# One split of the output weights, four quarter passes, and a norm bank of its own

## The chip, the cores and the metric

The kernel runs on one core of one Trainium2 chip. The metric is the device time of one execution in microseconds. The kernel before takes 2251.65 us, the median of three runs (2248.07 to 2252.68). The engines are called by their usual names: TensorE (PE) multiplies matrices, VectorE (DVE), ScalarE (ACT) and GpSimd (POOL) work on elements, and SyncE (SP) issues most of the transfers.

## The reference, cut to what matters

It is one layer of a decoder for 1024 prompt tokens and 8 sample tokens, model width 1024, feed-forward width 2816:

```
mix = (sigmoid(ga) * y_a + sigmoid(gb) * y_b) @ w_o
x   = x + gt1 * mix
h2  = rmsnorm(x, norm2_w) * (1 + sc2) + sh2
gate, up = h2 @ w_ffn_gate, h2 @ w_ffn_up
gc  = causal_dwconv3(gate with its state) + ffn_conv_b
x   = x + gt2 * ((silu(gc) * up) @ w_ffn_down)
y   = rmsnorm(x, final_norm_w)
```

Ahead of these lines come the modulation from the conditioning, one combined input projection, a gated delta rule (its output times w_gdn_out is y_a) and sliding-window attention (its output times w_swa_out is y_b). All numbers are float32.

## The kernel before

Every matrix lies transposed on the chip, channels on the 128 partitions and tokens along the row, so a matrix of width 1024 is 8 blocks of channels. To keep float32 accuracy, every operand is split in a high part, rounded by ScalarE (`split`, L126), and a low part, the rest, from VectorE (L127); a product is three matmuls (`mm3`, L168 high by high, L169 high weight by low operand, L170 low weight by high operand). A weight block is 1024 rows by 128 columns: `load_w` loads its 512 KB into one of three buffers called raw and splits it in two tiles of 128x1024.

The tokens are cut in three parts for the branches (`PARTS`), and in four quarters of 256, 256, 260 and 260 columns behind them (`QUARTERS`); quarters 0 and 1 are one half, 2 and 3 the other (`HALF`). The stage around the change goes like this.

`branches` ends with the eight products by w_gdn_out. The evacuation of each (L1224, L1225) gives the mixed branch, split by quarters into tiles bmh0 and bml0 to bmh3 and bml3. For the first two blocks the loop goes over parts outside and blocks inside, for the others block by block.

`output_pass` multiplies by w_o: for each of the eight blocks j it loads and splits the weights, loads the residual x, multiplies (24 matmuls for a quarter), adds the gated product into x1 (`add_gated`, L1312 to L1317), squares x1 on ScalarE (L1288), adds the squares up on GpSimd (L1292), and stores x1 to memory as x1d for the end of the layer. It runs three times: once with quarters 0 and 1 together, then for quarter 2 and for quarter 3. So w_o is loaded and split three times; in the last two, the low parts of blocks 2, 4 and 6 are made by GpSimd.

`second_norm` norms one quarter: small matmuls with a column of ones sum the squares over partitions (L1335), VectorE scales (L1336), GpSimd takes the power -1/2 (L122), VectorE makes diagonal blocks (L1342), matmuls with ones spread them over the partitions (L1343), VectorE multiplies x1 with them (L1347), and ScalarE applies scale and shift (L1353; the 8 sample tokens on VectorE, L1350 and L1351). Its two PSUM tiles are those called wy, which the feed-forward uses too.

`operands` makes from the two quarters of a half the seven operands of a product in the manner of Strassen and Winograd: the differences at L1375, two on VectorE and two on GpSimd, then seven splits. The first half's operands go to tiles pk0 to pk6, the second's to the bm tiles. `pair_weights` makes the seven weights for two column blocks of the feed-forward; its four sums are GpSimd's (L1420). `ffn_gate_up` multiplies, for f = 0, first with the first half alone, then with the second; for later f it takes both halves product by product. A product's result is kept by ScalarE (L1454) or added by VectorE (L1497, L1527).

The order of the work on each engine is set by the framework's priorities. `weave` gives each stream a start and a step: `(first, 30, 34)` says that a stream begins 30 places behind the current priority and that each of its steps comes 34 later. Within that, the framework's scheduler sorts instructions by priority and by when its own model has their inputs ready; each engine then works its list strictly in order. SP's list holds loads and stores in one queue.

At the end, `ffn_rows` and `last_norm` write the convolution's state rows and the normed output; both put their scratch into one buffer called fth (L1621).

## Time and profile before

| | |
|---|---|
| median of three runs | 2251.65 us |
| the profiled execution | 2246.54 us |
| its span, first to last instruction | 2244.8 us |
| mean granted clock of TensorE | 0.966 |
| busy: TensorE, VectorE, ScalarE, GpSimd | 2126.8, 1348.2, 817.4, 380.3 us |

In a row of the profile, L1312 is a line of the kernel before, `out<-in` are the tiles by their names without numbers, x8 a count. A row of a timeline gives the start in the span and the duration in us; the square bracket holds how long the engine had stood idle and what released it. A row of waits gives the total, the number and the longest. The granted clock is a share of full speed. The stage of the change lies between 1378 us, where the last w_gdn_out product ends, and 1564 us, where the first column pair of the feed-forward is done.

### The profile page before, as it was taken

To read this page: it belongs to the slowest core of one execution; us is meant where nothing else is said; L and a number is where in the kernel's file an instruction comes from. 1 tells how busy PE (TensorE), PEld (TensorE's weight loads), DVE (VectorE), ACT (ScalarE), POOL (GpSimd) and SP (SyncE) were. 2 spreads that over 40 slices of the span, in tenths; PEclk is the share of its full clock that TensorE was granted. 3 is DMA by queue.
4 is the path that set the end of the run, shared out by engine and by line. 5 is a ranking of instruction groups with operands and counts; after the bars stand their busy time and mean duration, and the time that the engine had idled before them with its cause. 6 is when DMAs were issued, how large, how long until landed. Compare 5 with 4: busy or idle time off the path is not lost.

```text
span 2244.8 us, 41406 instructions
## 1 busy us (share of the span) xinstructions
PE 2126.8 (95%) x16565; PEld 1998.6 (89%) x16565; DVE 1348.2 (60%) x2877; ACT 817.4 (36%) x2049; POOL 380.3 (17%) x438
## 2 busy tenths in 40 slices
PE   7998999898999999999969999888999999999998
PEld 3796888698999999999859999888999999999997
DVE  4557666574465574564332764578776867856546
ACT  3445545423333433434330132444333433512102
POOL 2000000112112112122110200354333333100000
PEclk8999999799999999999969999999999999999999
DMA  9412322332223132133562846452222222353202
GB/s 338 135 40 74 122 82 95 91 78 59 71 65 88 56 77 70 53 88 97 158 197 91 250 121 186 120 144 77 84 78 84 76 95 67 128 194 123 86 1 79
DMA packets 285395, 236.55 MB, mean 105 GB/s; under 512 B 57534, under 2 KB 247905, under 8 KB 285186
## 3 DMA queue, kind: packets, MB, share of 16 engines
q1 hardware_dynamic: 282722, 229.09, 33.1%
q10 hardware_dynamic: 2304, 4.23, 0.5%
q8 instruction: 130, 2.13, 0.4%
q14 instruction: 63, 0.52, 0.1%
q0 software_dynamic: 176, 0.59, 0.1%
HBM read 183.90 MB, written 52.35 MB: 105 GB/s over the span
## 4 chain that ended last, share of the span: by engine, by line
PE 84%; DVE 6%; DMA 4%; ACT 3%; issue 2%; SPq 1%; POOL 0%; DVEq 0%; POOLq 0%; ACTq 0%
PE mm L168 18%; PE mm L170 18%; PE mm L169 18%; PE wv L169 3%; PE wv L170 3%; PE wv L168 3%; PE wy L168 2%; PE wy L169 2%; PE wy L170 2%; PE pv L600 1%; PE mm L252 1%; PE pt L178 1%; PE pv L598 1%; DMA b1l<-dlr 1%; PE tp L178 1%
## 5 line engine op out<-in xcount | busy, mean ns | idle before, releaser
L168 PE MATMUL mm<-b1h,wh 128*128 128x384 f32 (+1 forms) x1440 | 475.2, 331 | 9.2 <-DVE kx L496 4.5
L170 PE MATMUL mm<-b1h,wl 128*128 128x384 f32 (+1 forms) x1440 | 468.7, 326 | 3.8 <-DVE wl L127 3.7
L169 PE MATMUL mm<-b1l,wh 128*128 128x384 f32 (+1 forms) x1440 | 468.3, 326 | 0.1
L168 PEld LDWEIGHTS mm<-b1h,wh 128*128 128x128 f32 x1440 | 273.6, 190 | 22.0 <-issue 6.3
L169 PEld LDWEIGHTS mm<-b1l,wh 128*128 128x128 f32 x1440 | 274.0, 190 | 8.7 <-issue 7.1
L170 PEld LDWEIGHTS mm<-b1h,wl 128*128 128x128 f32 x1440 | 273.6, 190 | 6.5 <-DVE wl L127 4.6
L170 PE MATMUL mm<-bmh,w 128*128 128x260 f32 (+1 forms) x520 | 151.0, 291 | 8.2 <-POOL w L127 4.7
L168 PE MATMUL mm<-bmh,w 128*128 128x260 f32 (+1 forms) x520 | 150.7, 290 | 7.3 <-ACT w L126 6.8
L126 ACT ACTIVATE wh<-raw 128x1024 fp32r<-128x1024 f32 x77 | 80.7, 1048 | 157.3 <-PE mm L169 121.8
L168 PE MATMUL mm<-b2h,wh 128*128 128x384 f32 (+1 forms) x384 | 124.9, 326 | 1.0 <-DVE t L1220 0.9
L169 PE MATMUL mm<-b2l,wh 128*128 128x384 f32 (+1 forms) x384 | 124.5, 324 | 1.2 <-DVE b2l L127 1.2
L170 PE MATMUL mm<-b2h,wl 128*128 128x384 f32 (+1 forms) x384 | 123.8, 324 | 0.2 <-DVE wl L127 0.2
L127 DVE TENSOR_TENSOR wl<-raw,wh 128x1024 fp32r<-128x1024 f32 x76 | 93.9, 1235 | 43.9 <-ACT wh L126 42.9
L1312 DVE SCALAR_TENSOR_TENSOR x<-mm,mT,x 128x256 f32<-128x256 f32 (+2 forms) x133 | 63.4, 481 | 89.7 <-PE mm L170 83.7
L170 PEld LDWEIGHTS mm<-bmh,w 128*128 128x128 f32 x520 | 100.7, 194 | 10.7 <-POOL w L127 5.7
L168 PEld LDWEIGHTS mm<-bmh,w 128*128 128x128 f32 x520 | 100.8, 194 | 8.7 <-ACT w L126 7.9
L168 PE MATMUL mm<-pk,w 128*128 128x256 f32 x352 | 99.0, 281 | 1.7 <-ACT r L1454 1.7
L170 PE MATMUL mm<-pk,w 128*128 128x256 f32 x352 | 98.9, 281 | 0.1
L169 PE MATMUL mm<-pk,w 128*128 128x256 f32 x352 | 98.9, 281 | 0.0
L169 PE MATMUL mm<-bml,w 128*128 128x260 f32 (+1 forms) x344 | 98.8, 287 | 0.0
L126 ACT ACTIVATE w<-raw 128x512 fp32r<-128x512 f32 (+1 forms) x92 | 68.9, 752 | 74.0 <-PE mm L170 36.1
L127 DVE TENSOR_TENSOR w<-raw,w 128x512 fp32r<-128x512 f32 (+1 forms) x86 | 72.4, 843 | 27.9 <-ACT w L126 27.3
(571 smaller groups left out, 5815.5 us busy)
## 6 DMA issues: line engine op xcount, KB each, us to landing
raw<-in_w_in_dram SPq DMA_DIRECT2D x60, 512.0 KB
raw<-in_w_o_dram SPq DMA_DIRECT2D x24, 512.0 KB
bml<-act SPq DMA_DIRECT2D x22, 516.0 KB
raw<-in_w_ffn_gate_dram SPq DMA_DIRECT2D x22, 512.0 KB
raw<-in_w_ffn_up_dram SPq DMA_DIRECT2D x22, 512.0 KB
raw<-in_w_ffn_down_dram SPq DMA_DIRECT2D x22, 512.0 KB
qst<-in_w_mod_dram SPq DMA_DIRECT2D x16, 512.0 KB
raw<-in_w_mod_dram SPq DMA_DIRECT2D x16, 512.0 KB
```

The lines of the kernel that those rows point to most:

```text
L126: self.nc.scalar.activation(hi, x, AF.Copy)
L127: (eng or self.nc.vector).tensor_tensor(lo, x, hi.bitcast(F32), op=ALU.subtract)
L168: mm(ps, whi, xhi, start=first, stop=False, **kw)
L169: mm(ps, whi, xlo, start=False, stop=False, **kw)
L170: mm(ps, wlo, xhi, start=False, stop=last, **kw)
L178: self.nc.tensor.transpose(out, in_, self.ident[:p, :p])
L252: nc.tensor.matmul(ps[32 * j:32 * j + 32], self.cT[:, k0 + j, :], ws[j // 2][:, j % 2, :], start=k0 == 0, stop=k0 > 0)
L598: nc.tensor.matmul(out, V[:, n, ch], pc[:, r::2, :], start=True, stop=n == 0)
L600: nc.tensor.matmul(out, V[:, n - 1, ch], pp[:, r::2, :], start=False, stop=True)
L1312: nc.vector.scalar_tensor_tensor(x[:, :np_], ps[:, :np_], self.mT[:, m + j, 8:9], x[:, :np_], op0=ALU.mult, op1=ALU.add)
```

## The change

**Weights.** w_o is loaded and split once, in eight blocks (`output_weights`). Blocks 0 and 2 go to the weight tiles w0 to w3; the others to the tiles pk0 to pk5, which are operand rooms of the feed-forward. Block 0 is split in two halves of 512 columns, and its first product goes through all sixteen matmuls with the high weight first.

**Passes.** Four passes, one per quarter. x is loaded by quarter, in rows of 1024 or 1040 bytes per partition in place of 2048 or 2080. The three norms and operand streams are woven into the passes with starts of 250 (quarter 0), 490 (quarter 1) and 730 (quarter 2); the transposes of the feed-forward's states at 300. The first half's operands are bmh0, bml0, bmh1, bml1, pk6, pk0, pk1; the second's bmh2, bml2, pk2 to pk5, bmh3.

**Engines.** The sums of squares, all four differences of an operand stage, and the sums of the first column pair's weights are VectorE's; squares of the last quarter's last three blocks too. Squares of block 6 are not added to the sum but given to the norm as a third term.

**Norm.** A PSUM bank of its own, called nr; one VectorE instruction makes all diagonal blocks, and one matmul spreads them.

**Branches and tail.** Blocks 6 and 7 of w_gdn_out go part by part, like 0 and 1. The scratch of `ffn_rows` and `last_norm` lies in four buffers called ws.

What it moves on the engines, at the places that the prediction speaks of. First SP's list from the first residual load on in the kernel before (xT is the residual, x the tile x1, x1d its store):

```order
L1273 DMA x_2189_14273<-xT_10870 128x512 x7
L132 DMA raw_14472<-in_w_o_dram 128x8x128
L1273 DMA x_2189_14273<-xT_10870 128x512
L1273 DMA x_2190_14274<-xT_10870 128x520
L132 DMA raw_14538<-in_w_o_dram 128x8x128
L1273 DMA x_2190_14274<-xT_10870 128x520 x7
L1303 DMA x1d_14275<-x_2189_14273 128x512
L132 DMA raw_14604<-in_w_o_dram 128x8x128
L1303 DMA x1d_14275<-x_2189_14273 128x512
L132 DMA raw_14670<-in_w_o_dram 128x8x128
```

and in the change, from the first residual load behind three loads of w_o:

```order
L1302 DMA x_2189_14270<-xT_10870 128x256 x6
L1319 DMA raw_14384<-in_w_o_dram 128x8x128
L1302 DMA x_2189_14270<-xT_10870 128x256 x3
L1319 DMA raw_14420<-in_w_o_dram 128x8x128
L1312 DMA x1d_14272<-x_2189_14270 128x256
L1302 DMA x_2189_14270<-xT_10870 128x256
L1319 DMA raw_14456<-in_w_o_dram 128x8x128
L1302 DMA x_2189_14270<-xT_10870 128x256 x2
L1312 DMA x1d_14272<-x_2189_14270 128x256
L1302 DMA x_2189_14270<-xT_10870 128x256 x3
L1319 DMA raw_14492<-in_w_o_dram 128x8x128
```

A block's loads and stores now stand at distances of one quarter's product; a store (x1d) stands ahead of the loads of the blocks 5 and 6.

Second, VectorE behind the norm of the last quarter, before (x is x1 of the second half, wy the spread row, td a difference):

```order
L1347 TENSOR_TENSOR x_2190_14274<-x_2190_14274,wy_15615 128x4x260 x2
L1350 TENSOR_TENSOR x_2190_14274<-x_2190_14274,a_12354 128x4x8 x2
L1351 TENSOR_TENSOR x_2190_14274<-x_2190_14274,mT 128x4x8 x2
L1375 TENSOR_TENSOR x_2190_14274<-x_2190_14274 128x4x260
L1375 TENSOR_TENSOR td_15649<-x_2190_14274 128x1040
L127 TENSOR_TENSOR w_2416_15899<-raw_15894,w_2416_15899 128x512
L127 TENSOR_TENSOR bml_2372_15565<-x_2190_14274,bml_2372_15565 128x1040
L127 TENSOR_TENSOR bmh_2375_15568<-x_2190_14274,bmh_2375_15568 128x1040
L127 TENSOR_TENSOR bmh_2371_15564<-td_15649,bmh_2371_15564 128x1040
L127 TENSOR_TENSOR bmh_2373_15566<-x_2190_14274,bmh_2373_15566 128x1040
L127 TENSOR_TENSOR bml_2374_15567<-x_2190_14274,bml_2374_15567 128x1040
```

and in the change (nr is the spread row):

```order
L1373 TENSOR_TENSOR x_2190_14271<-x_2190_14271,nr_15518 128x4x260 x2
L127 TENSOR_TENSOR w_2351_15798<-raw_15793,w_2351_15798 128x512
L1376 TENSOR_TENSOR x_2190_14271<-x_2190_14271,a_12354 128x4x8 x2
L1377 TENSOR_TENSOR x_2190_14271<-x_2190_14271,mT 128x4x8 x2
L1400 TENSOR_TENSOR x_2190_14271<-x_2190_14271 128x4x260
L1400 TENSOR_TENSOR td_15541<-x_2190_14271 128x1040
L1400 TENSOR_TENSOR x_2190_14271<-x_2190_14271 128x4x260
L127 TENSOR_TENSOR pk_2311_15471<-x_2190_14271,pk_2311_15471 128x1040
L1400 TENSOR_TENSOR x_2190_14271<-x_2190_14271,td_15541 128x4x260
L127 TENSOR_TENSOR bmh_2314_15474<-x_2190_14271,bmh_2314_15474 128x1040
L127 TENSOR_TENSOR pk_2310_15470<-td_15541,pk_2310_15470 128x1040
```

All four differences (L1375 before, L1400 now, where two of them were GpSimd's) now stand in this list, each as soon as its inputs are there, with the splits between them; one weight split stands between scaling and sample columns.

Third, TensorE in the first column pair, where it comes to operands of the second half that need both quarters, before (the last three rows are the first product with bml1, made from a difference):

```order
L168 MATMUL mm_15674<-pk_2360_15508,w_2388_15606 128x256
L169 MATMUL mm_15674<-pk_2360_15508,w_2388_15606 128x256
L170 MATMUL mm_15674<-pk_2360_15508,w_2388_15606 128x256
L168 MATMUL wv_15824<-bml_2372_15565,w_2384_15596 128x260
L169 MATMUL wv_15824<-bml_2372_15565,w_2384_15596 128x260
L170 MATMUL wv_15824<-bml_2372_15565,w_2384_15596 128x260
```

and in the change, where pk_2311 and pk_2310 are such operands:

```order
L168 MATMUL mm_15573<-pk_2299_15395,w_2326_15510 128x256
L169 MATMUL mm_15573<-pk_2299_15395,w_2326_15510 128x256
L170 MATMUL mm_15573<-pk_2299_15395,w_2326_15510 128x256
L168 MATMUL wv_15723<-pk_2311_15471,w_2322_15500 128x260
L168 MATMUL mm_15680<-pk_2310_15470,w_2321_15497 128x260
L169 MATMUL wv_15723<-pk_2311_15471,w_2322_15500 128x260
L170 MATMUL wv_15723<-pk_2311_15471,w_2322_15500 128x260
```

In the lists, the norm's sums of the last quarter (L1335, now L1360) stand 24 matmuls of products behind the last w_o product before, and 44 behind it in the change; from there to the product with the first operand of both quarters are 72 more before, and 52 in the change.

The diff, cut (left out: removed lines, and the new names of buffers in the tail):

```diff
--- before.py
+++ after.py
@@ -1248,12 +1248,16 @@
         self.bm = self.pool("bm", 1, side="right")
         self.mix = [tuple(self.t(self.bm, [P, KC, QW], f"bm{x}{q}", F32R)[:, :, :n] for x in "hl")
                     for q, (_, n) in enumerate(QUARTERS)]
...
+        for j0 in (0, 2, 4, 6):
+            w = [self.load_w(I["w_gdn_out"][0][:, j * P:(j + 1) * P]) for j in (j0, j0 + 1)]
+            if 0 < j0 < 6:
+                for j in (j0, j0 + 1):
+                    self.project(w[j - j0], oa, ya_out)
+                continue
+
+            for t in range(3):
+                for j in (j0, j0 + 1):
+                    self.project(w[j - j0], oa, ya_out, (t,))
 
     def gate_part(self, pool, src, t):
         s = self.t(pool, [P, 384], "sgx", bufs=3)[:, :PARTS[t][1]]
@@ -1263,45 +1267,65 @@
 
     def pair_tiles(self, p):
 
...
+        tags = ("bmh2", "bml2", "pk2", "pk3", "pk4", "pk5", "bmh3") if p else \
+            ("bmh0", "bml0", "bmh1", "bml1", "pk6", "pk0", "pk1")
+        return [self.room(tag, [P, KC, QW]) for tag in tags]
+
+    def room(self, tag, shape):
+        pool = self.bm if tag[0] == "b" else self.pk if int(tag[2]) < 4 else self.pk2
+        return self.t(pool, shape, tag, F32R)
+
+    def output_pass(self, pool, q):
+
+        nc = self.nc
+        lo, n = QUARTERS[q]
+        x1 = self.x1[q // 2][:, :, lo - HALF[q // 2][0]:][:, :, :n]
 
         def add(t, ps):
             self.add_gated(t, ps, j, 16)
...
+            sq = self.t(pool, [P, QW], "nsq" if j else "nss", bufs=3 if j else 2)[:, :n]
+            if q == 3 and j > 4:
+                nc.vector.tensor_tensor(sq, x1[:, j, :], x1[:, j, :], op=ALU.mult)
+            else:
+                nc.scalar.activation(sq, x1[:, j, :], AF.Square)
             if j == 0:
...
+                self.squares[q] = [sq]
+            elif j < 6:
+                s = self.squares[q][0]
+                nc.vector.tensor_tensor(s, s, sq, op=ALU.add)
             else:
...
+                self.squares[q].append(sq)
 
         for j in range(8):
...
+            if q == 0:
+                self.wo.append(self.output_weights(j))
+            nc.sync.dma_start(x1[:, j, :], self.xT[j][:, lo:lo + n])
+            if q or j:
+                self.project(self.wo[j], self.mix, add, parts=(q,), cols=QUARTERS)
+            else:
+                ps = self.t(self.next_mm(), [P, 512], "mm")[:, :n]
+                (wh, wl), (xh, xl) = self.wo[0], self.mix[0]
+                for i in range(3 * KC):
+                    w, x, k = (wh, (xh, xl)[i % 2], i // 2) if i < 2 * KC else (wl, xh, i - 2 * KC)
+                    nc.tensor.matmul(ps, w[:, k, :], x[:, k, :], start=i == 0, stop=i == 3 * KC - 1)
+                add(0, ps)
+            nc.sync.dma_start(self.x1d[j][:, lo:lo + n], x1[:, j, :])
             yield
+
+    def output_weights(self, j):
+
+        src = self.I["w_o"][0][:, j * P:(j + 1) * P]
+        raw = self.t(self.pw, [P, NP], "raw", bufs=3)
+        self.nc.sync.dma_start(raw.rearrange("p (k c) -> p k c", k=KC), src.rearrange("(k p) c -> p k c", p=P))
+        if j in (0, 2):
+            w = [self.t(self.pw, [P, NP], tag, F32R, bufs=1) for tag in (f"w{j}", f"w{j + 1}")]
+        else:
+            room = self.room(("pk0", "", "pk1", "pk2", "pk3", "pk4", "pk5")[j - 1], [P, KC * QW])
+            w = room[:, :NP], room[:, NP:2 * NP]
+        for c in (0, 512) if j == 0 else (slice(None),):
+            c = c if j else slice(c, c + 512)
+            self.split(*(x[:, c] for x in w), raw[:, c])
+        return [x.rearrange("p (k c) -> p k c", k=KC) for x in w]
 
     def add_gated(self, t, ps, j, m):
@@ -1327,20 +1351,22 @@
         nc_ = (n + P - 1) // P
         rs = self.t(pool, [P, 4], "rs", bufs=2)
         nc.vector.memset(rs, 1.0)
...
+        r = self.t(psum, [P, 512], "nr", bufs=1)
+        ss = r[:, 384:388]
+        sqs = self.squares[t]
         for c in range(nc_):
             w = min(P, n - c * P)
...
+            for i, sq in enumerate(sqs):
+                nc.tensor.matmul(ss[:w, c:c + 1], sq[:, c * P:c * P + w], self.ones[:, 0:1], start=i == 0,
+                                 stop=i == len(sqs) - 1)
+        for w, c0, c1 in ((P, 0, 2), (n - 2 * P, 2, nc_)):
+            if c0 < c1:
+                nc.vector.tensor_scalar(rs[:w, c0:c1], ss[:w, c0:c1], 1.0 / NP, EPS, op0=ALU.mult, op1=ALU.add)
         self.power(rs[:, :nc_], rs[:, :nc_], self.mhalf)
         yield
...
+        dg = self.t(pool, [P, 3, P], "dg", bufs=1)[:, :nc_]
+        nc.vector.tensor_tensor(dg, bc(self.ident, 1, nc_), bc(rs[:, :nc_], 2, P), op=ALU.mult)
+        nc.tensor.matmul(r[:, :n], self.ones, dg.rearrange("p c i -> p (c i)")[:, :n], start=True, stop=True)
         yield
         for k0 in (0, 4):
             xk = x[:, k0:k0 + 4, :]
@@ -1371,16 +1397,21 @@
             yield
             return
         d = self.t(pool, [P, 4, QW], "td", bufs=1)[:, :, :n]
-        v, g = self.nc.vector, self.nc.gpsimd
-        minus = lambda e, out, x, y: e.tensor_tensor(out, x, y, op=ALU.subtract)
-        minus(v, a1, b1, a1)
-        minus(v, d, b2, a1)
+        minus = lambda out, x, y: self.nc.vector.tensor_tensor(out, x, y, op=ALU.subtract)
+        minus(a1, b1, a1)
+        self.split(*ops[3], a1)
         yield
-        minus(g, b1, b2, b1)
-        minus(g, a2, a2, d)
-        for op, x in zip(ops[2:], (d, a1, b1, a2, b2)):
-            self.split(*op, x)
-            yield
+        minus(d, b2, a1)
+        self.split(*ops[2], d)
+        yield
+        minus(b1, b2, b1)
+        self.split(*ops[4], b1)
+        yield
+        minus(a2, a2, d)
+        self.split(*ops[5], a2)
+        yield
+        self.split(*ops[6], b2)
+        yield
 
 
     def ffn_states(self, pool, psum):
@@ -1403,9 +1434,10 @@
             nc.vector.tensor_tensor(out, st[:, :m, :, 0], bc(fcw[:, 0, c0:c0 + m], 2, NS), op=ALU.mult)
             nc.vector.tensor_tensor(tmp[:, :m], st[:, :m, :, 1], bc(fcw[:, 1, c0:c0 + m], 2, NS), op=ALU.mult)
             nc.vector.tensor_tensor(out, out, tmp[:, :m], op=ALU.add)
+            yield
         nc.vector.tensor_tensor(sp, sp, bc(fcw[:, 3, :], 2, NS), op=ALU.add)
 
-    def pair_weights(self, pool, w, f):
+    def pair_weights(self, pool, w, f, eng=None):
 
 
         raw = []
@@ -1416,8 +1448,8 @@
         n = [0]
 
         def calc(x, y, op):
-            s = self.t(pool, [P, 4, P], "ws", bufs=4)
-            self.nc.gpsimd.tensor_tensor(s, x, y, op=op)
+            s = self.t(self.pw, [P, 4, P], "ws", bufs=4)
+            (eng or self.nc.gpsimd).tensor_tensor(s, x, y, op=op)
             return s
 
         def put(x):
@@ -1518,7 +1550,7 @@
 
         for pairs in ((0,), (1,)) if first else ((0, 1),):
             self.pair_product(pool, psum, w, pairs, gate)
-        w = self.pair_weights(pool, I["w_ffn_up"][0], f)
+        w = self.pair_weights(pool, I["w_ffn_up"][0], f, nc.vector if first else None)
 
         def up(p, i, q, ps, r):
             lo, n = QUARTERS[2 * p + q]
@@ -1644,20 +1676,21 @@
             with S() as right:
                 xr = self.pool("xr", 1, ctx=right, side="right")
                 with S() as left:
...
+                    xl = self.pool("xl", 1, ctx=left)
                     self.x1 = [self.t(pl, [P, KC, n], "x1") for pl, (_, n) in zip((xl, xr), HALF)]
                     self.x1d = self.t(self.dr, [KC, P, NT], "x1d")
...
+                    self.squares, self.X, self.wo = {}, {}, []
+                    norm = lambda q: self.second_norm(xr, psum, q)
+                    self.weave((chain(*(self.output_pass(xr, q) for q in range(4))), 0, 1),
+                               (self.ffn_states(xr, psum), 300, 30),
+                               (chain(norm(0), self.operands(xr, 0, 0)), 250, 10),
+                               (chain(norm(1), self.operands(xr, 0, 1)), 490, 20),
+                               (chain(norm(2), self.operands(xr, 1, 0)), 730, 120))
                 with S() as left:
                     pool = self.pool("pf", 1, ctx=left)
...
+                    w = self.pair_weights(pool, self.I["w_ffn_gate"][0], 0, nc.vector)
+                    last, ops = norm(3), self.operands(xr, 1, 1)
+                    self.weave((chain(islice(last, 3), islice(ops, 1), last, ops), -100, 1))
                     right.close()
                     with S() as right2:
                         pool2 = self.pool("pa", 1, ctx=right2, side="right")
...
```

61 lines of the change are left out of this document (4 added, 57 removed).

## The prediction

> **What bounds the kernel now.** I read the page first: the busy shares, and the span in 40 slices of 56.1 us. The last two rows quoted are TensorE's busy tenths and its granted clock.
>
> ```profile
> span 2244.8 us, 41406 instructions
> PE 2126.8 (95%) x16565; PEld 1998.6 (89%) x16565; DVE 1348.2 (60%) x2877; ACT 817.4 (36%) x2049; POOL 380.3 (17%) x438
> ...
> PE   7998999898999999999969999888999999999998
> ...
> PEclk8999999799999999999969999999999999999999
> ```
>
> TensorE is the bound (2126.8 us busy of the span of 2244.8), so a change pays only where TensorE stands still, runs at a lower clock or does needless work. Three neighbouring slices are at 8: they are 1403 to 1571 us, the stage that the change rewrites. Next, the table of stretches. Its columns: stretch; length; busy us (instructions) of TensorE, its weight loads, VectorE, ScalarE, GpSimd; granted clock; DMA share; GB/s.
>
> ```profile
> 1378.00:1403.00 25.00, 21.99 (x172) 21.58 (x171) 10.43 (x18) 7.76 (x13) 4.09 (x4) 0.93 0.89 287
> 1403.00:1429.00 26.00, 26.00 (x226) 25.86 (x225) 8.37 (x13) 6.61 (x12) 8.43 (x9) 1.00 0.21 69
> 1429.00:1466.00 37.00, 27.82 (x188) 25.52 (x186) 31.58 (x40) 23.48 (x35) 20.42 (x10) 0.86 0.52 150
> 1466.00:1503.00 37.00, 32.80 (x261) 31.43 (x262) 25.02 (x46) 20.09 (x32) 17.46 (x14) 1.00 0.63 179
> 1503.00:1530.00 27.00, 16.70 (x115) 15.06 (x114) 23.13 (x26) 14.84 (x25) 18.60 (x12) 0.85 0.23 69
> 1530.00:1564.00 34.00, 33.53 (x261) 33.23 (x261) 32.10 (x53) 12.95 (x26) 11.97 (x13) 0.92 0.17 54
> 1564.00:1604.00 40.00, 40.00 (x338) 40.00 (x338) 29.57 (x54) 15.85 (x32) 13.70 (x12) 1.00 0.33 107
> ```
>
> The first six rows are the stage: the joint pass (two rows), quarter 2, quarter 3, the start of the feed-forward, the rest of its first column pair. They last 186.0 us. The seventh row is the next column pair, undisturbed: 40.00/338 = 0.118 us per matmul of 256 or 260 columns. The stage's products are 4 quarters x 8 blocks x 24, and 336 for the column pair: 1104 matmuls, 130.6 us. TensorE is busy 158.8 of 186.0, so 27.2 us are idle. The clock takes (0.07x25 + 0.14x37 + 0.15x27 + 0.08x34) = 13.7 us. What is left, 186.0 - 130.6 - 27.2 - 13.7 = 14.5, is norms, transposes of states and edges. So at most 55 us are to be had. The same stretch by waits (TensorE, in total, times, longest) and two rows of the chain of waits:
>
> ```profile
> PE mm L168 <- ACT w L126: 6.8, 5, 2.5
> PE wv L169 <- DVE bml L127: 6.0, 1, 6.0
> PE mm L170 <- POOL w L127: 4.7, 4, 1.9
> PE mm L170 <- DVE w L127: 3.4, 4, 1.7
> 1429.25 4.45 DMA raw<-in_w_o_dram
> 1433.79 1.06 ACT w L126
> ```
>
> 14.9 us wait for a split weight block: a load of 4.45 us, 1.06 on ScalarE, then its low part. The 6.0 is one wait for the last quarter's operands.
>
> **VectorE and GpSimd.** These groups of the stage (count, busy, mean ns) carry the prices:
>
> ```profile
> L127 DVE TENSOR_TENSOR w<-raw,w 128x1024 fp32r<-128x1024 f32 x18 | 22.6, 1260 | 7.4 <-ACT w L126 6.9 <-DMA x<-xT 0.5
> L127 DVE TENSOR_TENSOR pk<-x,pk 128x1024 fp32r<-128x1024 f32 x6 | 13.3, 2235 | 0.0
> L1375 DVE TENSOR_TENSOR td<-x 128x1024 f32<-128x1024 f32 x1 | 3.3, 3290 | 0.0
> L127 POOL TENSOR_TENSOR w<-raw,w 128x1024 fp32r<-128x1024 f32 x6 | 16.7, 2790 | 10.1 <-ACT w L126 10.1
> L1375 POOL TENSOR_TENSOR x<-x 128x1040 f32<-128x1040 f32 x1 | 3.5, 3459 | 1.5 <-ACT w L126 1.5
> L1292 POOL TENSOR_TENSOR nss<-nss,nsq 128x260 f32<-128x260 f32 x12 | 13.9, 1155 | 10.0 <-ACT nsq L1288 9.2 <-PE wy L1343 0.7
> L1292 POOL TENSOR_TENSOR nss<-nss,nsq 128x256 f32<-128x256 f32 x12 | 12.5, 1044 | 145.4 <-ACT nsq L1288 145.4
> 1509.43 1.28 POOL L1420 TENSOR_TENSOR ws<-ws,raw 128x512 f32<-128x512 f32 x1
> 1508.05 0.67 DVE L127 TENSOR_TENSOR w<-ws,w 128x512 fp32r<-128x512 f32 x1
> ```
>
> The same subtraction of 1024 columns takes 1.26 us in one group and 2.24 in another, and a difference 3.29: both of the latter while GpSimd worked. The Trainium skill ("SBUF — State Buffer", Who interferes with whom) says that a VectorE instruction with two SBUF inputs and a GpSimd one that reads SBUF lock each other out for a whole instruction. By that rule the stretch goes wholly with GpSimd's work; by the rows alone it could stay; the trace agrees with the rule in size (3.29 is 1.2 and about 2).
>
> **The change part by part.**
>
> (a) Weights. 16 of 24 loads and splits go: 6 on GpSimd, 10 on VectorE. Passes 1 to 3 wait for no weight, so 14.9 us of waits shrink to those of the first block. There, half a block is split first; I put 2.2 us from the last product of the branch to the first of w_o, and 0.5 for one low part (before: 25.00 - 21.99 = 3.0). Bounds: 1 and 5.
>
> (b) VectorE's bill. Off: 10 x 1.26 = 12.6. On: 20 sums of squares and 3 squares of 260 columns at about 0.4 (under the 0.67 of 512) = 9.2, 4 differences at 1.24 = 5.0, 8 pair sums at 0.67 = 5.4. Net +7.0. Against it the stretch: 6 x (2.24 - 1.24) = 6.0 on the operands, 2.0 on the difference, some 7 in the last chain (below). The six rows sum to 130.6 us, so about 123 in some 159: 77%, below TensorE. GpSimd (81.0 in the six rows) loses 16.7 + 26.4 + about 22 of differences (4 at about 3: rows at 3.46 here and 2.83 under (d)) and sums (8 at 1.28). A VectorE sum costs 0.4 to 0.7 where a product lasts 24 x 0.118 = 2.8; that cover is thin in the last pass alone, where operands of quarters 0 to 2 are made as well: 22 to 26 us of VectorE work, counted in the changed order, beside 24.
>
> (c) The own norm bank, one ones-matmul per norm and 256-wide loads of x: a norm matmul no longer waits for a bank of the feed-forward's. I cost norms and transposes at 9 (before 14.5 with edges); bounds 6 and 14. The loads are as many bytes in twice as many pieces, on the same queue; they are due one pass later.
>
> (d) The last chain. Before, from the last w_o product's sum to the first product on the last quarter's operands:
>
> ```profile
> 1502.71 0.48 DVE L1312 SCALAR_TENSOR_TENSOR x<-mm,mT,x 128x252 f32<-128x252 f32 x1
> 1507.60 1.85 POOL L122 TENSOR_TENSOR rs<-rs,mhalf 128x3 f32<-128x3 f32 x1 [2.88 <-DVE rs L1336]
> 1509.49 2.53 DVE L1342 TENSOR_SCALAR dg<-ident,rs 128x128 f32<-128x128 f32 x2 [0.77 <-POOL rs L122]
> 1515.00 2.38 DVE L1347 TENSOR_TENSOR x<-x,wy 128x1040 f32<-128x1040 f32 x2
> 1516.27 4.02 ACT L1353 ACTIVATE x<-x,mT,a 128x252 f32<-128x252 f32 x8
> 1517.30 2.18 DVE L1350 TENSOR_TENSOR x<-x,a 128x32 f32<-128x32 f32 x2
> 1520.81 1.24 DVE L1375 TENSOR_TENSOR x<-x 128x1040 f32<-128x1040 f32 x1
> 1525.60 2.83 POOL L1375 TENSOR_TENSOR x<-x,td 128x1040 f32<-128x1040 f32 x1
> 1526.11 3.41 DVE L127 TENSOR_TENSOR bml<-x,bml 128x1040 fp32r<-128x1040 f32 x1
> 1529.58 0.58 PE L169 MATMUL wv<-bml,w 128*128 128x260 f32 x1 [5.99 <-DVE bml L127]
> ```
>
> That is 26.9 us. In the change, counted from the end of the last w_o product: 44 matmuls of products stand ahead of the norm's sums and 39 more ahead of the row matmul, 9.8 us; with the sums and the matmul it ends near 11.0 (sums at 5.2, scale, power and diagonal some 2.5 in between: hidden by the products). Scaling on ScalarE starts 1.27 later (L1347 to L1353) and lasts 4.0: 16.3. The first difference falls inside, two more follow at 1.24 each: 18.8. ScalarE's high parts of bmh3 and pk2, in that order, are 1.06 each, and sample columns 0.3: 21.2. TensorE has 96 such matmuls and the norm's own matmuls as cover, 12.7 us, then waits 8.5 for pk2, and 1.2 more for its low part: 9.7 in all, where 10.3 + 0.5 stood before (27.00 - 16.70, 34.00 - 33.53). So the chain is shorter by 5, but its cover shrinks almost as much. Bounds: 4 if the scaling is met earlier, 16 if VectorE is 6 us behind.
>
> (e) Pair 6,7 of the branch by token parts: the same matmuls, at full clock before and after. The next block's loads are issued earlier. 0, bounds -1 and +1.
>
> (f) The tail. Squares of the last norm get four buffers. Before:
>
> ```profile
> PE wv L178 <- DVE raw L1629: 3.5, 2, 2.2
> ACT fth L1621 <- PE wy L178: 2.3, 1, 2.3
> ```
>
> The first is a wait for banks, which stays in part. 1.5, bounds 0 and 4.
>
> **The sum.** 130.6 of products, 2.7 in (a), 9.7 in (d), 9 in (c), 1.4 for the stretch's edges (0.4 before, 1.0 behind), and clock: (a) keeps the first row's 1.75, (d) the fifth row's 4.05, 5.8 together. 159.2, against 186.0: 26.8 less; with the tail 28.3, taken as 28. The profiled execution's time, 2246.54 (1.74 over its span), becomes 2218.5; it lies 5.1 under the median of the runs, 2251.65, to which I apply the same difference: **2224**. What a change of 0.2% (4.5 us) or less does can't be told from none here.
>
> **Rivals.**
>
> R1, VectorE becomes the bound in the last pass and behind it: 26 of work in 24, with evacuations queued behind operand subtractions, then the chain starts late and (d) is 16: 6 + 2 + half of a clock dip, 9 to 10 less gained: 2233. For: 77% busy on average and the order has operand splits next to sums. Against: the seventh row runs at full clock with VectorE at 29.57 of 40.00, 74%.
>
> R2, pass 0 is bound by loads.
>
> ```profile
> raw<-in_w_o_dram SPq DMA_DIRECT2D x24, 512.0 KB
> ```
>
> A block (524 kB), its piece of x and its store (131 each) are 0.79 MB in 2.8 us, 280 GB/s; the first stretch shows 287 at a share of 0.89. A store waits at the head of SP's queue for its product's sum, and the next blocks' loads stand behind it. Load, high and low part are 4.45 + 1.06 + 1.26 = 6.8 us for a room of three buffers, due every 8.4. If the load took 8 us, five blocks would each be 0.6 late, and with a store's wait 1 to 1.5: 5 to 8 us, 2231.
>
> R3, the chain is met earlier and the clock holds: (d) 4, clock 1.75, norms 7: 12 more gained, 2212.
>
> R4, slower: VectorE is stretched everywhere as in the second group, 2.24 for 1.24. Its 123 us become 222, more than the stage's 186, and the time 2251.65 + 36, with a late start some 2290. It decides from a mean stretch of 1.5 on (123 x 1.5 = 185). For: VectorE takes over GpSimd's work one for one and is in the chain behind every product. Against: what is left on GpSimd is four powers, the second column pair's sums at 1.28, some 16 us in all, and in the seventh row, with 13.70 of GpSimd's work, TensorE loses nothing.
>
> R5, the weights can't stay: the rooms are also operands' rooms, and were one taken before its last product, operands 0 and 1 would wait for the end of pass 3. By the changed order the first pairs' operands go to quarters' rooms that are free after their own pass. If not, half of (a) is lost, 2237.
>
> **How the numbers follow.** The forecast 0.62 (its own range 2217 to 2231), R1 0.15, R2 0.07, R3 0.09, R4 0.05, R5 0.02. Cases other than R4 are all more than 4.5 us faster, but R1 and R5 together could eat nearly all: 0.02 for the same. Faster 0.93, slower 0.05. The range: upward R1 with bounds of (c) added, 2239; downward R3 within 1, 2213.
>
> **What would show it.** Right: in passes 1 to 3 no wait of TensorE for w, a pass's 192 matmuls in about 24 us, VectorE's operand subtractions near 1.25, one wait of 7 to 11 us on pk2 or pk3 some 13 us behind the last w_o product, the first clock dip after it. Wrong: waits for raw or x in pass 0 (R2), evacuations that end passes 2 and 3 late (R1), subtractions above 2 (R4). I would be wrong in (d) if the norm's sums came to TensorE much earlier or later than 44 matmuls behind the last product.

## The result, and the profile after

The changed kernel takes 2234.29 us (median of 4 runs, 2233.41 to 2238.49) where the kernel before took 2249.89 beside it (4 runs, 2248.07 to 2252.68): the ratio is 0.9933, with an interval of 0.9915 to 0.9951. A second set of runs gave 2233.25 against 2249.11, ratio 0.9932 (0.9911 to 0.9953). So the change is worth 15.6 us in the first set and 15.9 in the second; the forecast was 28.

Two rows of the page of the profile after: TensorE's busy tenths and its granted clock. Of the three neighbouring slices at 8, none is left; a new one at 8 stands in the 36th place, at 1950 to 2010 us.

```profile
PE   7998999899999999999979999999999999989998
...
PEclk8999999799999999999979999999999999989999
```

To see where the time went, I cut both traces at the same events: the last w_gdn_out sum, the last w_o sum, the last sum of the first column pair, the last sum of the feed-forward, and the 32nd sum of the down projection. The columns are those of the table of stretches in the prediction. First the kernel before: the w_o passes, the first column pair, the start of the down projection.

```profile
1378.58:1502.71 124.13, 107.78 (x834) 103.77 (x835) 75.12 (x114) 57.94 (x92) 50.14 (x34) 0.95 0.56 170
1502.71:1563.21 60.50, 49.74 (x369) 47.79 (x368) 54.77 (x77) 27.15 (x50) 30.84 (x25) 0.89 0.19 58
1967.04:2015.68 48.64, 43.93 (x347) 43.72 (x347) 22.46 (x54) 5.21 (x6) 0.00 (x0) 0.93 0.55 202
```

The same three of the changed kernel:

```profile
1381.04:1491.08 110.04, 108.01 (x846) 104.50 (x847) 67.69 (x133) 44.95 (x80) 2.57 (x3) 0.97 0.42 126
1491.08:1546.60 55.52, 47.47 (x366) 46.06 (x365) 44.90 (x74) 23.36 (x44) 12.62 (x14) 0.91 0.13 38
1949.18:2004.08 54.90, 45.52 (x359) 45.31 (x358) 24.86 (x56) 7.37 (x8) 0.00 (x0) 0.88 0.54 193
```

| stretch, us | before | changed | difference | forecast |
|---|---|---|---|---|
| w_o passes and first column pair | 184.6 | 165.6 | -19.0 | -26.8 |
| rest of the feed-forward and start of the down projection | 452.5 | 457.5 | +5.0 | 0 |
| from there to the end | 229.1 | 227.6 | -1.5 | -1.5 |
| sum, from the last w_gdn_out sum to the end | 866.2 | 850.7 | -15.5 | -28.3 |

The first event itself lies 2.5 us later in the changed kernel's span. Over the fourteen profiles of this case it lies anywhere from 1375.5 to 1389.4, with the same work ahead of it, so below I compare profiles from that event to the end (866.2 before, 850.7 changed) and times by their medians.

TensorE's waits between 1378 and 1548 us in the changed kernel:

```profile
PE wv L168 <- ACT pk L126: 4.8, 1, 4.8
PE mm L1310 <- ACT w L126: 2.1, 1, 2.1
PE mm L168 <- ACT pk L126: 1.3, 1, 1.3
PE mm L168 <- ACT fz L1527: 1.1, 1, 1.1
PE mm L169 <- DVE pk L127: 0.7, 1, 0.7
```

The waits for split blocks are gone but for the first (L1310 is the product that takes the high weight first). In 166 us TensorE is idle for 2.0 + 8.1 us, where it was 16.3 + 10.8. So the waits fell as forecast. Yet the stretch is 7.8 us longer than the forecast, while TensorE stands in it as busy. That, and the 5 us at the start of the down projection, are what the experiments are for.

### The profile page after: what moved, and what is told of

The parts are those of the page before. It is cut to its first block, busy times and chain, and to the rows that moved or that the text cites. A ratio compares the mean times of both kernels' runs of the same rounds, so it can differ in the third digit from the quotient of the medians.

```text
span 2231.7 us, 41326 instructions
## 1 busy us (share of the span) xinstructions
PE 2122.2 (95%) x16573; PEld 1995.1 (89%) x16573; DVE 1333.0 (60%) x2893; ACT 800.1 (36%) x2031; POOL 311.7 (14%) x396
## 4 chain that ended last, share of the span: by engine, by line
PE 84%; DVE 6%; DMA 5%; ACT 2%; SPq 2%; issue 1%; POOL 0%; DVEq 0%; POOLq 0%; ACTq 0%
PE mm L168 18%; PE mm L169 18%; PE mm L170 18%; PE wv L169 3%; PE wv L170 3%; PE wv L168 3%; PE wy L168 2%; PE wy L170 2%; PE wy L169 2%; PE pv L600 1%; PE mm L252 1%; PE pv L598 1%; PE pt L178 1%; DMA b1l<-dlr 1%; PE tp L178 1%
## 5 line engine op out<-in xcount | busy, mean ns | idle before, releaser
L168 PE MATMUL mm<-pk,w 128*128 128x260 f32 (+1 forms) x440 | 124.5, 283 | 1.3 <-ACT pk L126 1.3
L169 PE MATMUL mm<-pk,w 128*128 128x260 f32 (+1 forms) x440 | 124.3, 283 | 0.7 <-DVE pk L127 0.7
L170 PE MATMUL mm<-pk,w 128*128 128x260 f32 (+1 forms) x440 | 124.4, 283 | 0.0
L168 PE MATMUL mm<-bmh,pk 128*128 128x260 f32 (+1 forms) x362 | 105.0, 290 | 9.4 <-DVE x L1336 9.4
L170 PE MATMUL mm<-bmh,pk 128*128 128x260 f32 (+1 forms) x362 | 103.3, 285 | 0.0
L169 PE MATMUL mm<-bml,pk 128*128 128x256 f32 (+1 forms) x335 | 95.7, 286 | 0.0
L168 PE MATMUL mm<-bmh,w 128*128 128x260 f32 (+1 forms) x320 | 91.4, 286 | 1.1 <-ACT fz L1527 1.1
L170 PE MATMUL mm<-bmh,w 128*128 128x260 f32 (+1 forms) x320 | 91.7, 287 | 0.0
L1486 ACT COPY r<-mm 128x256 f32<-128x256 f32 (+1 forms) x132 | 49.2, 374 | 113.4 <-PE mm L170 93.1
L127 DVE TENSOR_TENSOR w<-ws,w 128x512 fp32r<-128x512 f32 x88 | 61.3, 698 | 43.7 <-ACT w L126 43.7
```

The lines of the kernel that those rows point to most:

```text
L127: (eng or self.nc.vector).tensor_tensor(lo, x, hi.bitcast(F32), op=ALU.subtract)
L168: mm(ps, whi, xhi, start=first, stop=False, **kw)
L169: mm(ps, whi, xlo, start=False, stop=False, **kw)
L170: mm(ps, wlo, xhi, start=False, stop=last, **kw)
L1486: nc.scalar.copy(r[p, i], x[p])
```

## What the busy time holds: small matmuls between large ones

Two sets of groups of TensorE, before and changed (count, busy us, mean ns). L178 are the transposes of the feed-forward's states, L1335 and L1360 the norms' sums, L1343 and L1369 the spreading matmuls. Before:

```profile
L1343 PE MATMUL wy<-dg,ones 128*128 128x128 f32 x16 | 3.5, 325 | 1.4 <-DVE dg L1342 1.4
L1335 PE MATMUL wy<-ones,nsl 128*128 128x1 f32 x16 | 2.8, 245 | 0.0
L1335 PE MATMUL wy<-ones,nss 128*128 128x1 f32 x16 | 2.5, 228 | 0.3 <-DVE rs L1336 0.3
L178 PE MATMUL wv<-ident,raw 16*128 16x16 f32 x22 | 1.7, 210 | 0.0
```

Changed:

```profile
L178 PE MATMUL wv<-ident,raw 16*128 16x16 f32 x22 | 4.8, 233 | 0.0
L1360 PE MATMUL nr<-ones,nsq 128*128 128x1 f32 x32 | 4.6, 232 | 0.0
L1360 PE MATMUL nr<-ones,nss 128*128 128x1 f32 x16 | 2.6, 229 | 0.0
L1369 PE MATMUL nr<-dg,ones 128*128 128x256 f32 x4 | 1.5, 449 | 0.0
L1369 PE MATMUL nr<-dg,ones 128*128 128x260 f32 x4 | 1.2, 382 | 0.0
```

The transposes take 4.8 us of busy time in place of 1.7, though they are the same 22. What differs is their place. Before, they stood in packs between two passes; now the stream of states is woven in between products, and the timeline shows one transpose, one product, one transpose:

```profile
1412.85 0.23 PE L178 MATMUL wv<-ident,raw 16*128 16x16 f32 x1
1413.01 0.38 PE L168 MATMUL mm<-bmh,pk 128*128 128x256 f32 x1
1413.33 0.23 PE L178 MATMUL wv<-ident,raw 16*128 16x16 f32 x1
1413.49 0.38 PE L169 MATMUL mm<-bml,pk 128*128 128x256 f32 x1
1413.80 0.23 PE L178 MATMUL wv<-ident,raw 16*128 16x16 f32 x1
```

From transpose to transpose (1413.33 to 1413.80) it is 0.47 us, and the product between them is worth 0.117. A lone transpose thus costs 0.35 us. Added up in this way (from the start of the product ahead to the start of the product behind, less 0.117), the 22 cost 7.3 us, where they cost 1.7 before; the norms' small matmuls come to about 6.4, where they were 7.4. None of it shows as idle time. What follows in the clock:

```profile
1416.00:1422.00 6.00, 6.00 (x37) 4.85 (x36) 1.56 (x7) 0.42 (x1) 0.58 (x1) 1.00 0.43 109
1422.00:1426.00 4.00, 4.00 (x21) 3.53 (x20) 3.01 (x5) 2.25 (x5) 0.00 (x0) 0.58 0.37 109
1432.00:1438.00 6.00, 6.00 (x53) 6.00 (x53) 4.86 (x10) 0.84 (x2) 0.00 (x0) 1.00 0.28 100
```

37 matmuls in 6 us, then a stretch at 0.58 of the clock without any wait ahead of it, then 53 in 6 us. The Trainium skill ("TensorE: Matmul & The Clock Gate", HAM oscillation — how this bites in real kernels) ties the drop to gaps in which TensorE is idle for more than some 3.4 us; here the dip follows a stretch that the trace shows as wholly busy, with small matmuls in it. Whether the gate saw these as idle, the trace can't show.

## The experiments

The first question is which part earned the 19 us. Theories: the weights (no waits for splits), or the engines (GpSimd no longer stretches VectorE). All experiments but one (the engines alone) start from the changed kernel.

**Weights reloaded** in the last two passes:

```diff
+            if q > 1:
+                self.wo[j] = self.load_w(self.I["w_o"][0][:, j * P:(j + 1) * P],
+                                         tags=("w2", "w3") if j % 2 else ("w0", "w1"))
             if q or j:
```

> The changed kernel, but in the passes of quarters 2 and 3 every w_o block is loaded and split again into two alternating pairs of tiles, as before the change; all else as changed. Weights theory (the gain of the stage is the waits for a split block, 14.9 us before, and their clock): 10 to 16 us slower than the changed kernel, near 2247, with waits of TensorE for w in both passes of 10 us or more. Engine theory (the gain is that GpSimd no longer stretches VectorE): 0 to 4 us slower, near 2236, and few such waits, since loads and splits are unhindered now.

Measured: 2242.29 us (10 runs, 2236.16 to 2246.59; ratio to before 0.9966, 0.9951 to 0.9981), 8.0 slower than the changed kernel; in the profile 858.7, 8.0 more. TensorE's waits:

```profile
PE wv L168 <- ACT pk L126: 6.3, 1, 6.3
PE mm L170 <- DVE w L127: 3.9, 4, 2.5
PE mm L1313 <- ACT w L126: 2.1, 1, 2.1
PE mm L168 <- ACT w L126: 1.6, 2, 1.4
```

By the time, this is between the two expectations, and the waits for reloaded blocks are 5.5 us, not 10. But the run changed a second thing. Its transposes no longer stand one by one: they lie in three packs of 8, 8 and 6, late in the passes. The passes, and the first pack:

```profile
1375.90:1491.52 115.62, 106.91 (x846) 104.47 (x846) 78.70 (x137) 56.72 (x90) 3.28 (x3) 0.96 0.61 182
1480.92 0.66 PE L178 MATMUL wv<-ident,raw 16*128 16x16 f32 x8
```

The first two passes are 8.6 us shorter than in the changed kernel (50.9 against 59.5), the last two 14.2 longer (64.7 against 50.5). So the 8.0 us are a loss less a gain. (The states and the reloaded blocks go through the same buffers, raw; that this is what moves the transposes is argued, not shown.) Like is compared with like against the run with late transposes below, which keeps the weights and has packs too: there reloading costs 13.7 us by the medians of one set of runs, with intervals that lie apart, and 14.1 in the profile. Of this 12.8 lie in the passes, 6.7 as idle time. That is the weights theory's size, though not its 10 us of waits.

**Sums and differences on GpSimd again**, the weights kept:

```diff
-                nc.vector.tensor_tensor(s, s, sq, op=ALU.add)
+                nc.gpsimd.tensor_tensor(s, s, sq, op=ALU.add)
...
-        minus(b1, b2, b1)
+        minus(b1, b2, b1, self.nc.gpsimd)
...
-        minus(a2, a2, d)
+        minus(a2, a2, d, self.nc.gpsimd)
...
-                    w = self.pair_weights(pool, self.I["w_ffn_gate"][0], 0, nc.vector)
+                    w = self.pair_weights(pool, self.I["w_ffn_gate"][0], 0)
```

(and the same for the sums of w_ffn_up).

> The changed kernel, but the sums of squares, two differences of each operand stage and the first column pair's weight sums are GpSimd's again. Engine theory: 6 to 12 us slower than the changed kernel, VectorE's operand subtractions near 2 us again and a longer wait on the last quarter's operands. Weights theory: 0 to 4 us slower, all of it in the last chain, because in passes 1 to 3 VectorE's work has cover.

Measured: 2238.80 us (5 runs, 2232.40 to 2245.59; ratio 0.9957, 0.9933 to 0.9982), 4.5 slower, in the profile 4.2. The runs scatter so far that this is within their intervals. VectorE's subtractions for operands, in this run:

```profile
L127 DVE TENSOR_TENSOR pk<-x,pk 128x1024 fp32r<-128x1024 f32 x3 | 6.8, 2250 | 0.5 <-ACT pk L126 0.5
L127 DVE TENSOR_TENSOR bmh<-x,bmh 128x1040 fp32r<-128x1040 f32 x2 | 4.7, 2334 | 0.0
```

and in the changed kernel:

```profile
L127 DVE TENSOR_TENSOR pk<-x,pk 128x1024 fp32r<-128x1024 f32 x3 | 3.7, 1223 | 0.4 <-ACT pk L126 0.3
L127 DVE TENSOR_TENSOR bmh<-x,bmh 128x1040 fp32r<-128x1040 f32 x2 | 2.5, 1232 | 0.0
```

The stretch is real, and comes and goes with GpSimd's work, as the prediction had it (2.25 against 1.22 us; the Trainium skill's rule in "SBUF — State Buffer", Who interferes with whom, agrees). But it is nearly all off the path: TensorE is idle for the same 2.0 us in the passes, and 9.1 against 8.1 behind them. The passes are longer (114.8 against 110.0) at a clock of 0.94, but so they are in one profile of a kernel whose code is the same there (115.1 at 0.94, below).

**Both undone:**

> The changed kernel with both parts undone: w_o loaded and split again in the passes of quarters 2 and 3, and the sums and two differences on GpSimd. If weights and engines add up (8.0 and 4.5 us alone): 12 to 13 us slower than the changed kernel, near 2247, so that next to nothing is left of the gain. If they are one thing, for instance because VectorE is stretched only while it also splits weights: 16 us or more slower. If either part alone already spoils the same cover: 8 to 9 us slower, near 2243.

Measured: 2242.53 us (7 runs, 2237.41 to 2244.72; ratio 0.9964, 0.9952 to 0.9977), in the profile 859.3: the third case, 8 us and not 12. With the weights reloaded, the engines add nothing (2242.53 against 2242.29). The transposes are in packs here too (8 and 14), so that against the run with late transposes the loss is some 14 us. And some 7 us of gain over the kernel before are still there.

**The engines alone, from the kernel before:** the same three moves there.

> The kernel before, with one part of the change alone: sums of squares, the two differences and the sums of the first column pair's weights on VectorE. VectorE's subtractions for operands fall from 2.24 to 1.25 us and some 14 us of stretch go from VectorE either way. Theory that this stretch was on the path (the 6.0 us wait for the last operands, 4.7 for low parts of weights): 5 to 9 us faster than before, near 2242. Rival, that weight loads cover it and the moved work stands in VectorE's list ahead of weight splits: within 2 us of before.

Measured: 2245.88 us (10 runs, 2239.70 to 2253.60) against 2249.11, ratio 0.9986 (0.9974 to 0.9999); in the profile 862.5 against 866.2. 3 us, between the two. (The profile is of the slowest of its ten executions.) The operands' subtractions fell to 1.21 us, and the wait for the low part of the last operands from 6.0 to 1.6; with the wait for their high part (0.9, now 1.7) that is 6.9 to 3.3. The waits for split blocks only changed places: 14.9 before, 14.8 now.

```profile
PE mm L168 <- ACT w L126: 7.4, 5, 2.6
PE mm L170 <- DVE w L127: 5.7, 4, 3.4
...
PE mm L170 <- POOL w L127: 1.7, 3, 1.0
PE wv L169 <- DVE bml L127: 1.6, 1, 1.6
```

The waits for GpSimd's low parts fell from 4.7 to 1.7, those for VectorE's rose from 3.4 to 5.7 and those for ScalarE's high parts from 6.8 to 7.4. That fits the rival, by which work moved onto VectorE stands ahead of weight splits; it is not shown apart.

**Nearly all undone:** weights reloaded with the low parts of blocks 2, 4 and 6 on GpSimd, sums and differences on GpSimd, blocks 6 and 7 of w_gdn_out block by block, and the norm in the feed-forward's banks:

```diff
-        r = self.t(psum, [P, 512], "nr", bufs=1)
+        r = self.t(psum, [P, 512], "wy", bufs=2)
```

> The changed kernel with nearly all undone: w_o reloaded in quarters 2 and 3 with the low parts of blocks 2, 4 and 6 on GpSimd, sums and two differences on GpSimd, the norm in the feed-forward's banks wy, and blocks 6 and 7 of w_gdn_out block by block. What is left is the order (four passes and where norms and operands stand in them) and the one ones-matmul. Theory that the rest of the gain is those GpSimd low parts and the norm's bank: within 2 us of the kernel before, the stage near 182. Rival, that it is the order: near 2242, the stage near 175.

Measured: 2250.89 us (10 runs, 2247.23 to 2258.76), ratio to before 1.0009 (0.9996 to 1.0023); the two stretches of the stage are 182.7 us (in a profile of the slowest of the ten executions). The first theory holds: what is left of the change, the order of four passes above all, is together worth nothing, though the transposes stand in packs here too (8, 8 and 6). The 8.4 us between this and the run with both undone belong to GpSimd's low parts, the bank and the branch's last blocks, which I did not separate.

As a chain of medians, then (from three sets of runs, in which the kernel before took 2248.23 to 2249.48): from nearly all undone, 8.4 us for these three parts, 0.2 for the engines, 13.7 for the weights kept, and 5.7 lost again, because the changed kernel's transposes are scattered, as the next run shows. The weights are the largest part.

The second question is the mis-sized stretch. **Transposes late**, by one number; in the order they then stand in three packs of 7, 6 and 9, now in passes 2 and 3 in place of pass 1:

```diff
-                               (self.ffn_states(xr, psum), 300, 30),
+                               (self.ffn_states(xr, psum), 1000, 30),
```

> The changed kernel, but the stream of the 22 small transposes of the feed-forward's states starts at priority 1000 in place of 300; they then stand in few packed groups in passes 2 and 3. Theory that scattered transposes cost passes 0 and 1 about 4 us and a stretch of half clock: 2 to 4 us faster. Rival: they cost the same wherever they stand, and their loads hold buffers that the feed-forward's weights need: 0 to 3 us slower.

Measured: 2228.58 us (4 runs, 2225.65 to 2235.22; ratio to before 0.9916, 0.9892 to 0.9939), 5.7 faster than the changed kernel by the medians, with intervals that overlap; in the profile 844.6, 6.1 less. The passes of w_o, the first column pair, and the transposes:

```profile
1384.37:1487.16 102.79, 100.77 (x839) 99.95 (x840) 60.07 (x114) 41.48 (x74) 2.72 (x3) 0.98 0.38 115
1487.16:1545.21 58.05, 50.08 (x378) 47.90 (x379) 54.00 (x93) 27.16 (x51) 14.44 (x14) 0.91 0.23 71
...
L178 PE MATMUL wv<-ident,raw 16*128 16x16 f32 x22 | 1.9, 211 | 0.0
...
1456.89 0.60 PE L178 MATMUL wv<-ident,raw 16*128 16x16 f32 x7
```

Seven in a pack are busy for 0.60 us and cost the stream 0.62, where one alone cost 0.35; all 22 cost 1.9, where they cost 7.3. The passes are 7.2 us shorter, more than the 2 to 4 expected: 5.4 are the transposes', and most of the rest goes with the clock (0.98 against 0.97). The idle time in the passes is 2.0 us in both: the whole gain lies in time that the profile called busy. The first column pair is 2.5 us longer. VectorE makes eight sums of weights there, none in the changed kernel, and waits 1.6 us for a load of w_ffn_gate, as the rival said; but TensorE is idle there for 8.0 us as against 8.1, and 12 more matmuls stand in the stretch, so how much of the 2.5 is lost is open.

**Two terms of squares** for the norm, as before the change (`elif j < 7` for `elif j < 6`): 20 of the 60 sums' instructions go.

> The changed kernel, but the norm gets two terms of squares as before: block 6 is added on VectorE, and 20 of the 60 small matmuls of the norms' sums go. Theory that each costs TensorE about 0.12 us: the passes of w_o and the first column pair are 2 to 3 us shorter. Rival (they fall into time that TensorE has anyway, and one VectorE sum more per norm stands in the last chain): no change, or up to 1 us slower.

Measured: 2230.25 us (4 runs, 2225.14 to 2234.09; ratio 0.9913, 0.9894 to 0.9932), 4.0 faster by the medians, with intervals that overlap; in the profile 850.4 against 850.7, at a clock of 0.95 against 0.97 in the passes. Inconclusive: the 2 to 3 us that were looked for are no larger than the scatter of the clock.

That scatter has a run of its own, **the changed kernel once more:**

> The changed kernel itself, run and profiled once more beside the next three. The stretch from the last w_gdn_out sum to the last w_o sum took 110.0 us in its first profile and 115.1 in that of the run with x1's loads on GpSimd's queue, whose code is the same there. If this is scatter of the granted clock: a time near 2234, that stretch anywhere from 109 to 116 with the difference in its clock (0.97 against 0.94), and its start in the span moved by some us, with no instruction changed ahead of it. If the queue did it: 110 within 1.

Measured: 2233.25 us (8 runs, 2226.75 to 2244.45), the passes 110.8 us at a clock of 0.97. The 115.1 us of the run below stand at 0.94 and with 1.6 us more idle:

```profile
1383.21:1498.34 115.13, 111.52 (x846) 107.65 (x847) 68.05 (x134) 44.54 (x80) 2.57 (x3) 0.94 0.40 120
```

Scatter, then: with the same code in the passes, three profiles agree (110.0, 110.8, and 111.0 in the run with rooms below) and one is some 5 us longer. For this kernel, a single profile decides nothing under 5 us in the passes.

The third question is the start of the down projection, where x1 is loaded again and the first sums wait for it. **x1's loads on GpSimd's queue** (`nc.gpsimd.dma_start` for `nc.scalar.dma_start`):

> The changed kernel, but the 16 loads that bring x1 back for the down projection are issued by GpSimd, which has nothing else there, and not from ScalarE's list, where splits that wait for loads stand ahead of them (issued 7.3 us behind the last store of the feed-forward, against 0.9 before the change). Queue theory: TensorE's wait on the first sums of the down projection falls from 9.4 to 3 to 6 us and the kernel gains 3 to 6 us. Transfer theory (the transfers are saturated there and the bytes set the time): 0 to 1 us.

Measured: 2236.43 us (4 runs, 2229.69 to 2238.68; ratio 0.9941, 0.9919 to 0.9964): no gain. The loads were issued 0.1 us behind the last store, where ScalarE's list issued them 5.3 to 6.8 behind it, but TensorE still waits:

```profile
PE mm L168 <- DVE x L1336: 7.6, 1, 7.6
```

against 9.4 and 8.0 in the two profiles of the changed kernel. The queue theory falls.

**Rooms in the order of release**, for weights and activations:

```diff
+        rooms = [[(pool_of(tag), tag) for tag in tags] for tags in (
+            ("bmh0", "bml0", "bmh1", "bml1", "pk6", "pk0", "pk1"),
+            ("bmh2", "bml2", "pk2", "pk3", "pk4", "pk5", "bmh3"))]
```

> The changed kernel, but the down projection puts its split weights and activations into the operand rooms in the order in which the changed feed-forward gives them back (first operands' rooms first, as it was before the change). Rooms theory (the change of rooms made the first blocks of the down projection wait for operands that are read last, so that loads bunch behind the feed-forward): the stretch from the feed-forward's last sum to the 32nd sum of the down projection falls from 54.9 to 48 to 50 us, the kernel gains 4 to 6. Rival (the feed-forward's end and the reload of x1 set it, and the transfers are saturated in any order): 0 to 1.5 us.

Measured: 2231.45 us (4 runs, 2228.60 to 2236.26; ratio 0.9924, 0.9903 to 0.9944). The stretch fell to 48.8 us as the theory said, but the feed-forward ahead of it grew from 402.6 to 406.6, because TensorE's list now holds more first products of the down projection among the last of the feed-forward (3410 matmuls in that stretch, against 3376); together 455.4, against 457.5 and 455.1 in the changed kernel's two profiles. The wait is 8.4 us. The event I had chosen moved; the rooms gained 2 us at most.

**The combination** of late transposes, rooms and two terms:

> The changed kernel with the late transposes, the rooms in the order of their release and two terms of squares together. If the three are independent: the 5.7 us of the late transposes, 4 to 6 of the rooms and 2 of the terms, 10 to 13 us faster than the changed kernel, near 2222. If rooms and terms do nothing: near 2229.

Measured: 2223.04 us (4 runs, 2220.14 to 2225.03; ratio to before 0.9881, 0.9867 to 0.9896), in the profile 840.1. That is 26.4 us faster than before, and its interval lies apart from the changed kernel's: 10 to 11 us better than it. The passes take 102.4 us, the first column pair 54.4. The passes' length is the sure part: 102.8, 102.4 and 102.3 us in the three profiles that keep the weights and pack the transposes (the third is the next run's), 110.0 to 115.1 in the six that keep the weights and scatter them (110.0, 110.8, 111.0, 111.9, 114.8, 115.1). The clock in the passes is 0.98 in each of the three and 0.94 to 0.97 in the six. So the scatter of the clock there goes with scattered transposes; why, the runs do not show. What rooms and two terms add, the runs do not tell apart.

**With the queue added:**

> The combined version (late transposes, rooms in the order of release, two terms) with x1's loads on GpSimd's queue too. If rooms and queue act on the same wait at the start of the down projection (5.1 us lost there by the change): 1 to 3 us faster than the combined version, near 2221, and TensorE's wait there near 5 to 6 in place of 8. If the transfers are saturated: no change from 2223.

Measured: 2222.69 us (4 runs, 2221.07 to 2223.17; ratio 0.9884, 0.9868 to 0.9901): the same. TensorE's wait at the start of the down projection is 11.7 us there, longer. What makes this wait 7.6 to 11.7 us in all kernels with the new passes and 4.7 and 5.1 in the two with the old ones (before, and engines alone) stays open: neither the queue nor the rooms alone, nor the two together, undo it. The 20 us around the wait, before and then in the changed kernel:

```profile
1970.00:1990.00 20.00, 15.29 (x107) 15.08 (x107) 7.54 (x16) 2.99 (x3) 0.00 (x0) 0.83 1.00 368
```

```profile
1953.00:1973.00 20.00, 10.62 (x66) 10.41 (x66) 7.84 (x16) 3.48 (x4) 0.00 (x0) 0.66 0.98 351
```

The transfers are busy for shares of 1.00 and 0.98, so saturated transfers would fit, but they are as busy before, so that this alone explains no difference; a kernel with fewer bytes there was not tried. Nor does the wait look like a gain that comes back: nearly all undone gains 1.9 us in the stage and still waits 10.9 there, and its stretch from the first column pair to the 32nd sum is 458.5 us against 452.5 before, while the combination gains 27.9 and loses 3.3.

## Why the prediction was right, and where it was wrong

The direction, and the range (2213 to 2239), held; the size was 28 and measured 15.6. That the time lies within the range is partly luck: 2234.29 is outside the forecast's own range (2217 to 2231) and beside R1's 2233, but R1 did not come. Step by step, for the profile from the last w_gdn_out sum on:

| step | forecast | measured | |
|---|---|---|---|
| products | 130.6 | 130.6 | the same 1104 matmuls |
| (a) first block | 2.7 | 2.0 | idle, 110.04 - 108.01 |
| (d) last chain | 9.7 | 8.1 | idle, 55.52 - 47.47 |
| clock | 5.8 | 8.3 | 0.03 x 110.04 + 0.09 x 55.52 |
| (c) norms, transposes | 9 | 16.6 | what is left of 165.6 |
| (f) tail | -1.5 | -1.5 | 229.1 to 227.6 |
| start of the down projection | none | +5.0 | 452.5 to 457.5 |

(a) held. In (d) the chain came out to a few tenths as far as the end of the scaling:

```profile
1491.08 0.47 DVE L1336 SCALAR_TENSOR_TENSOR x<-mm,mT,x 128x252 f32<-128x252 f32 x1
1501.72 0.60 PE L1369 MATMUL nr<-dg,ones 128*128 128x260 f32 x2
1503.64 4.01 ACT L1379 ACTIVATE x<-x,mT,a 128x252 f32<-128x252 f32 x8 [0.52 <-DVE x L1373]
1505.79 1.24 DVE L1400 TENSOR_TENSOR x<-x 128x1040 f32<-128x1040 f32 x1
1507.56 1.05 ACT L126 ACTIVATE pk<-x 128x1040 fp32r<-128x1040 f32 x1
1508.66 0.59 PE L168 MATMUL wv<-pk,w 128*128 128x260 f32 x1 [4.79 <-ACT pk L126]
1510.58 0.59 PE L168 MATMUL mm<-pk,w 128*128 128x260 f32 x1 [1.33 <-ACT pk L126]
```

The row matmul ends 11.2 us behind the last sum's start (forecast 11.0 from the product's end), scaling ends at 16.6 (16.3). The first difference fell inside the scaling, as forecast. The wait was put at pk2; most of it came one instruction earlier, at pk3, whose high part ScalarE makes only behind the scaling. Together the waits on pk2 and pk3 are 6.8 us, where 9.7 were forecast; 1.1 of the 8.1 idle is another wait (fz).

(b) held in its parts: the operands' subtractions went from 2.24 to 1.22, VectorE's busy time in the stage from 129.9 to 112.6 us (123 were forecast, so the bill was 10 too high), and R1 and R4 did not come. I gave the stretch no term of its own in the sum, and the runs bear this out: with the weights reloaded, moving the engines' work is worth nothing (8.0 against 8.6 us lost in the profile), in the kernel before 3 us, and with the weights kept 4.5, which is within the scatter.

The step that failed is (c): "I cost norms and transposes at 9 (before 14.5 with edges); bounds 6 and 14". It came out at 16.6, above its own bound. I counted the small matmuls as the program has them and took a lower cost for fewer bank waits. For the norms this went the right way (7.4 to about 6.4); for the transposes it did not. The order was at hand, and showed them spread one by one between products; the trace before showed them only in packs (22 in 1.7 us), and I carried this price over to places where it does not hold: there they cost 7.3. The run with late transposes shows the term: the passes lose 7.2 us when the same 22 stand in packs. My own sign, 192 matmuls of a pass in about 24 us, shows the place: counted on TensorE from first product to first product, passes 0, 1 and 2 took 24.5, 32.8 and 24.8 us, with all 22 transposes in pass 1; with late transposes pass 1 takes 24.2. The clock, 8.3 in place of 5.8, is the other term that is too low.

The second error is a step that I did not have: the end of the feed-forward was taken to move as a whole, with all behind it. The start of the down projection waits longer than before: the stretch loses 5.0 us in the first profile and 2.6 in the second. The cause is not settled, as said above; against the idea that a gain ahead comes back there speaks the run with nearly all undone, which loses 6.0 there with a gain of 1.9 ahead.

R2 (loads in pass 0) did not come: behind the first product, no wait there. R5 neither: the weights stayed.

## What to carry to other kernels

A small transpose, put alone between the matmuls of a stream, cost four times what it cost in a pack (0.35 us against 0.62 for seven), and the profile books that as busy; so when an order is woven finer, price the pieces at the place where they will stand, and look at matmuls per microsecond, not at the busy share. When one part of a change is undone, look whether the order of other parts moved with it: the run that reloaded the weights seemed to cost 8.0 us, because its transposes went into packs on their own, and against a kernel with packs it costs some 14. Taking away a stretch or a wait pays only where that engine's lateness reaches the bound one: here the doubled subtractions were mostly covered, and the weight loads were not. And a stretch far behind the change, which waits for transfers, should be given a term of its own: here it lost 2.6 to 5.0 us, for a reason that stayed open.
